# Mixer queries of the second block in reverse order, bias tiles read from one row per head, and masks, constants and first loads placed elsewhere

## The chip, the cores and the metric

The kernel runs on one core of one Trainium2 chip. The metric is the device time of one execution in microseconds, the median of several runs. A core has TensorE (PE, with its weight loads as PEld), VectorE (DVE), ScalarE (ACT), GpSimd (POOL) and SyncE (SP); each runs its own list of instructions in order. DMAs are issued here by SP (weights and some inputs), POOL (small tables, masks, bias tiles) and ACT (one vector table).

## The reference

The input x has 256 rows of 1024 columns. Two blocks follow each other, and each has two layers.

```python
def reference(x, ...):
    x = first_block(x, positions, ...)      # per layer: dilated + stick-breaking attention, gates, conv FFN (2816)
    return second_block(x, mem_2, ...)      # per layer: mixer, cross attention to 256 memory rows, squared-relu MLP (4096)
...
bias = table[t5_bucket(key_pos - query_pos)]            # 28 columns: 8 + 4 + 16 heads
adm  = chunk_id(spos)[None, :] <= chunk_id(tpos)[:, None]
score = einsum('bqhs,bqh->bqs', relu(q_idx . k_idx), w_idx)   # even mixer: picks 64 keys for each query
s = q . k * scale + bias                                 # then masked, softmax, times values
```

The mixer of the second block's layer 0 ("even") has four pairs of heads with a selection of keys (dsa) and two pairs of difference heads (diff); that of layer 1 ("odd") has eight pairs with a band mask and sinks. Every mixer head adds a bias that depends on key position minus query position alone.

## The kernel before

All activations are kept transposed, as tiles of 128 channels by 256 rows of x, and every weight matrix is cut into blocks of up to 512 KB by `plan()`, in the order of their use. `prep` (L188 to L207) loads a block on SP's queue into one of three `raw` buffers, and ACT (L201) and DVE (L202) split it into a high and a low half in fp32r (`w`, eight buffers). A projection is then three matmuls per 128x128 piece (`mm3`: high by high, low by high, high by low). `take` prepares up to `LEAD` blocks ahead of the one in use. The order on each engine is set by a list scheduler at build time (`schedule_with_timeline_sim`); `no_sync(later, earlier)` only forces an order on one engine.

The places that the change touches:

- **Start** (L371 to L404): SP loads x in four tiles, weight block 0 between them, then blocks 1 and 2, the identity `ident`, the masks `m_dil`, `m_sb`, `m_tri`; POOL loads positions, `invf`, `m_chunk`, `m_band`, `table`, `sink`, `lamv`. `Split.chunk` (L267 to L274) scales x by the norm's gain and splits it, ACT the high half and DVE the low. DVE also makes the rope tables from the positions (L616 to L634).
- **The bias table** (`relative_bias`, L639 to L656), called at step j = 1 of the up projection of the first block's layer 0 (L872): one matmul turns the 32x28 table and a one-hot tensor into `brel`, one row of 384 floats per head, which goes to DRAM (`brel_d`). Seven copies of four heads each (L654, paced by a POOL copy at L888 in steps j = 2 to 8) then write every row 128 times with a pitch of 385 into `skew_d`. A bias tile (L486) is a read of `skew_d` with pitch 384, so that partition p sees the row from offset 127 - p on.
- **Bias tiles** (`bias_tile`, L489): DVE adds the mask `m_chunk` (diff heads) or `m_band` (odd heads) to the tile (L494). Tag "bias" has three buffers, of which `m_sb` holds one until the first block's layer 1 has used it.
- **Queries**: `scaled` (L1018) takes a projection out of PSUM with one DVE multiply. Query positions 0 to 127 and 128 to 255 are handled as two tiles (`TILE`). `split_half` (L497) takes an attention result out of PSUM, ACT the high half (L498) and DVE the low (L499).
- **Selection** (`index_scores` L1073, `choose` L1101): weights `wi` (L1063), scores summed in `work` (L1081), then eight rounds of MAX8 and MATCH_REPLACE8 on DVE; `dsa_pair` adds the result to the bias (L1161).
- **Constants of the second block**: the lambda sums (L942) and four copies of the sinks (L953).

Of the kernel before, what the change touches and what calls it, by code (L numbers as in the profile page):

```python
# [19 lines left out]
P = 128  # L20
# [110 lines left out]
def net(ctx, tc, A, out):  # L131
# [116 lines left out]
    class Split:  # L248
# [19 lines left out]
        def chunk(self, k, src, gain, eng=None):  # L268

            if k % 2 == 0:  # L270
                self.new()
            t = self(k)
            act.activation(t[:, 0], src, AF.Copy, scale=gain)
            (eng or dve).scalar_tensor_tensor(t[:, 1], src, gain, f(t[:, 0]), op0=OP.mult, op1=OP.subtract)  # L274
# [122 lines left out]
    ident = const("ident", [P, P])  # L397
# [4 lines left out]
    m_sb = sb("bias", "m_sb")  # L402
    nc.sync.dma_start(m_sb, A["m_sb"])
    m_tri = const("m_tri", [P, 2, P])  # L404
# [190 lines left out]
    for c in range(8):  # L595
        h.chunk(c, x[c // 2][:, c % 2], vcol(V_MIX + c))
# [9 lines left out]
    m_chunk = const("m_chunk", [P, T], nc.gpsimd)  # L606
    m_band = const("m_band", [P, T], nc.gpsimd)
# [3 lines left out]
    lamv = cp.tile([P, 4, 64], F32, name="lamv")  # L611
    nc.gpsimd.dma_start(lamv, A["lambda"].partition_broadcast(P))
# [3 lines left out]
    dve.tensor_copy(posf, pos)  # L616
# [22 lines left out]
    def relative_bias():  # L639
        onehot = sb("p", "onehot", (512,))  # L640
        nc.gpsimd.dma_start(onehot[0:32], A["onehot"])
        ps = bank("ms", "brel", (512,), part=28)
        pe.matmul(ps, table, onehot[0:32], start=True, stop=True)
        brel = sb("p", "brel_s", (512,))
        dve.tensor_copy(brel[0:28], ps)
        bdram = dp.tile([28, 384], F32, name="brel_d")
        nc.gpsimd.dma_start(bdram, brel[0:28, 0:384])

        skew = dp.tile([28, P * 385], F32, name="skew_d")
        def copy(h0, n=4):  # L650
            src = bass.AP(tensor=bdram.tensor, offset=bdram.offset + h0 * 384, ap=[[384, n], [0, P], [1, 384]])
            dst = bass.AP(tensor=skew.tensor, offset=skew.offset + h0 * P * 385,
                          ap=[[P * 385, n], [385, P], [1, 384]])
            return nc.gpsimd.dma_start(dst, src).ins  # L654

        return skew, copy  # L656

    for l in range(DEPTH):
# [38 lines left out]
        if l == 0:  # L697
            nrm = first_sums()
        rc = nrm.cols(0)
# [140 lines left out]
        def residual(w, y, k, gains):  # L840
# [5 lines left out]
            def on_part(c, a, b):  # L846
# [3 lines left out]
                dve.tensor_tensor(t, x[c // 2][:, c % 2], a, op=OP.add)  # L850
# [16 lines left out]
        for j in range(11):  # L867
# [4 lines left out]
            if j == 1 and l == 0:  # L872
                skew, copy = relative_bias()
# [67 lines left out]
    for j in range(2):  # L941
        dve.tensor_tensor_reduce(lprod, lamv[:, 2 * j], lamv[:, 2 * j + 1], 1.0, 0.0, op0=OP.mult, op1=OP.add,  # L942
                                 accum_out=lsum[:, j:j + 1])
# [7 lines left out]
    for m in range(2):  # L951
        for i in range(2):
            dve.tensor_copy(sink4[:, :, 2 * m + i], sink[:, 8 * m:8 * m + 8])  # L953
# [68 lines left out]

    def even(h, nrm):
# [5 lines left out]
        qb, kb = [scaled(o0, r8, "qb")], [scaled(o1, rr, "kb")]  # L1029
# [25 lines left out]
        def index_queries(c):  # L1055
            qi.append(scaled(proj_t("ev_in", c, h), rr, "qi"))
# [7 lines left out]

        def diff_operands(c):
            qb.append(scaled(proj_t("ev_in", c, h), r8, "qb"))
            kb.append(scaled(proj_t("ev_in", c + 256, h), rr, "kb"))

        def dsa_operands(c):
            qa.append(scaled(proj_t("ev_in", c, h), r8, "qa"))  # L1070
# [39 lines left out]
        def diff_pair(hp):  # L1110
# [39 lines left out]
            split_half(on, o_all.pairs[hp][:, :, 0], o_all.pairs[hp][:, :, 1])  # L1150

        def dsa_pair(hp):
# [10 lines left out]
            for n, c in enumerate(COLS):  # L1163
# [9 lines left out]
            split_half(o, t[:, 0], t[:, 1])  # L1173

        pipeline([diff_pair(0), index_keys, "step", lambda: index_queries(776), "step", lambda: index_queries(1032),
                  lambda: diff_values(0), "step", lambda: diff_values(1), "step",
# [7 lines left out]
    def odd(h, nrm):  # L1184
# [5 lines left out]
        qs = [scaled(o1, r8, "qo")]  # L1190
# [7 lines left out]
        def more(j):  # L1198
            qs.append(scaled(proj_t("od_in", 256 * j, h), r8, "qo"))
# [7 lines left out]
        def pair(ch):  # L1207
# [20 lines left out]
            split_half(o, t[:, 0], t[:, 1])  # L1228
# [228 lines left out]
def shape_constants():  # L1457
# [15 lines left out]
    C["m_tri"] = np.stack([np.where(j >= i, -8.0, 0.0), np.full((P, P), -8.0)], axis=1).astype(f4)  # L1473
    C["m_chunk"] = np.where(s // 64 <= t // 64, 0.0, NEG).astype(f4)
# [25 lines left out]
```

## Time and profile before

| | |
|---|---|
| median of 3 runs | 1460.91 us (1459.95 to 1466.13) |
| profiled execution, its own time | 1462.57 us |
| its span | 1460.5 us, so 2.07 us lie outside it |
| PE busy | 1404.1 us, 96% of the span |
| DVE busy | 1015.4 us, 70% |
| ACT busy | 886.0 us, 61% |
| POOL busy | 34.2 us, 2% |
| granted clock of TensorE, mean | 0.988 |
| bytes moved by DMA | 241.62 MB, mean 165 GB/s |

The kernel's work is a row of stages. The first block's layer 0 runs from 0 to some 397 us, its layer 1 to some 767 us with the same program but for loads and set-up, and the two layers of the second block fill the rest. The engines' busy shares are means over all stages; waits are read stage by stage.

### The profile page before, as it was taken

The page shows a single profiled execution, that of the slowest core. Times are in us where ns is not written, and L with a number is a line of the kernel's source. Part 1 is how long each engine was busy: PE and PEld are TensorE (multiplying, and loading weights), DVE is VectorE, ACT ScalarE, POOL GpSimd, SP SyncE. Part 2 cuts the span into 40 slices and gives each one's busy share as a digit, 9 for nine tenths or more (in the row PEclk, how much of TensorE's full clock was granted, in tenths as well). Part 3 has the DMA queues.
Part 4 walks back from the last instruction along what each step waited for, and adds up shares of the span by engine and source line. Part 5 has one row for each costly group of instructions (what it writes and reads, how often), then busy time and mean ns, then how long its engine had stood idle before and what let it go on. Part 6 is the DMA issues. An engine that isn't in the chain of part 4 may idle for free.

```text
span 1460.5 us, 26250 instructions
## 1 busy us (share of the span) xinstructions
PE 1404.1 (96%) x9948; PEld 1274.4 (87%) x9948; DVE 1015.4 (70%) x2135; ACT 886.0 (61%) x1744; POOL 34.2 (2%) x63
## 2 busy tenths in 40 slices
PE   8999999799999999999999998899999999899997
PEld 6789999798888899999999987699989978699986
DVE  6555887567665659888867795687656876677554
ACT  7556665455565566666756656576656676576553
POOL 1000000100000000000000010000000010000000
PEclk9999999899999999999999999999999999999998
DMA  8533666576654345565665554156566534266662
GB/s 263 166 116 106 186 187 213 175 227 198 199 173 147 102 151 178 186 187 186 207 196 160 156 158 132 61 157 186 182 183 185 167 102 131 62 199 188 188 188 87
DMA packets 74447, 241.62 MB, mean 165 GB/s; under 512 B 11663, under 2 KB 16159, under 8 KB 74321
## 3 DMA queue, kind: packets, MB, share of 16 engines
q1 hardware_dynamic: 67568, 230.03, 50.8%
q0 software_dynamic: 6608, 9.74, 2.2%
q8 instruction: 78, 1.28, 0.4%
q14 instruction: 49, 0.39, 0.1%
q10 hardware_dynamic: 144, 0.19, 0.0%
HBM read 238.79 MB, written 6.60 MB: 168 GB/s over the span
## 4 chain that ended last, share of the span: by engine, by line
PE 85%; DMA 6%; DVE 4%; ACT 4%; issue 1%; SPq 0%; POOL 0%; DVEq 0%; ACTq 0%; POOLq 0%
PE mm L231 52%; PE mw L231 21%; DMA raw<-in_wt_dram 4%; PE ssum L427 2%; PE mo L231 1%; DVE w L202 1%; PE sd L734 1%; DMA skew_d<-brel_d 1%; ACT w L201 1%; PE pT L483 1%; PE pv L524 1%; PE sc L586 1%; PE sc L585 1%; PE pv L525 1%; PE pTd L483 1%
## 5 line engine op out<-in xcount | busy, mean ns | idle before, releaser
L202 DVE TENSOR_TENSOR w<-raw,w 128x512 fp32r<-128x512 f32 (+2 forms) x866 | 585.2, 685 | 336.2 <-ACT w L201 327.2
L201 ACT ACTIVATE w<-raw 128x512 fp32r<-128x512 f32 (+2 forms) x866 | 532.2, 625 | 424.4 <-PE mm L231 218.1
L231 PE MATMUL mm<-xh,w 128*128 128x256 f32 x5892 | 723.6, 283 | 20.5 <-DVE fa L885 13.4
L231 PEld LDWEIGHTS mm<-xh,w 128*128 128x128 f32 x5892 | 704.2, 189 | 37.4 <-issue 20.1
L231 PE MATMUL mw<-xh,w 128*128 128x512 f32 (+1 forms) x1832 | 329.3, 340 | 4.6 <-DVE mx L1164 2.5
L231 PEld LDWEIGHTS mw<-xh,w 128*128 128x128 f32 x1832 | 282.1, 189 | 47.7 <-DVE mx L1164 2.9
L231 PE MATMUL mm<-w,xh 128*128 128x512 f32 (+2 forms) x672 | 147.1, 372 | 7.2 <-ACT w L201 7.1
L231 PEld LDWEIGHTS mm<-w,xh 128*128 128x128 f32 x672 | 114.0, 191 | 30.7 <-ACT w L201 8.1
L978 ACT ACTIVATE xh<-x,vec 128x256 fp32r<-128x256 f32 x48 | 22.6, 501 | 11.5 <-DVE x L1333 11.0
L487 POOL DMA_DIRECT2D bias<-skew_d x28 | 15.1, 543 | 611.7 <-DVE nm L535 275.0
L880 ACT ACTIVATE ftt<-fa,vec 128x256 f32<-128x256 f32 x44 | 24.1, 595 | 8.1 <-DVE fa L875 6.9
L231 PE MATMUL mo<-xh,w 128*128 128x256 f32 x192 | 28.0, 288 | 0.5 <-ACT xh L498 0.5
L231 PEld LDWEIGHTS mo<-xh,w 128*128 128x128 f32 x192 | 24.4, 189 | 3.8 <-issue 1.2
L981 DVE SCALAR_TENSOR_TENSOR xh<-x,vec,xh 128x256 fp32r<-128x256 f32 x48 | 22.0, 480 | 1.1 <-ACT xh L978 1.1
L431 ACT ACTIVATE sq<-x 128x512 f32<-128x512 f32 x33 | 20.4, 618 | 2.4 <-DMA x<-in_xT_dram 2.1
L881 DVE SCALAR_TENSOR_TENSOR ftt<-fa,vec,ftt 128x255 f32<-128x255 f32 x44 | 20.9, 483 | 0.7
L882 DVE SCALAR_TENSOR_TENSOR ftt<-fa,vec,ftt 128x254 f32<-128x254 f32 x44 | 21.0, 477 | 0.0
L178 ACT ACTIVATE ftt<-ftt 128x512 f32<-128x512 f32 x22 | 13.9, 631 | 9.9 <-DVE ftt L882 9.9
L265 ACT ACTIVATE xh<-fa 128x512 fp32r<-128x512 f32 x22 | 13.7, 625 | 9.9 <-DVE fa L886 9.8
L734 PE MATMUL sd<-qTs 64*128 64x128 f32 (+1 forms) x96 | 18.8, 350 | 0.0
L438 DVE TENSOR_TENSOR sq<-sq 128x512 f32<-128x512 f32 x26 | 17.8, 686 | 0.0
L1332 DVE TENSOR_TENSOR y<-y,rstd 128x512 f32<-128x512 f32 (+1 forms) x25 | 14.5, 581 | 4.5 <-ACT rstd L178 4.4
(406 smaller groups left out, 1162.6 us busy)
## 6 DMA issues: line engine op xcount, KB each, us to landing
raw<-in_wt_dram SPq DMA_DIRECT2D x411, 512.0 KB, 3.6
raw<-in_wt_dram SPq DMA_DIRECT2D x16, 384.0 KB, 3.5
skew_d<-brel_d POOLq DMA_DIRECT2D x7, 768.0 KB, 16.2
bias<-skew_d POOLq DMA_DIRECT2D x28, 128.0 KB, 3.1
raw<-in_wt_dram SPq DMA_DIRECT2D x4, 520.0 KB, 3.5
mem<-in_memT_dram SPq DMA_DIRECT2D x8, 256.0 KB, 3.7
x<-in_xT_dram SPq DMA_DIRECT2D x4, 256.0 KB, 5.9
raw<-in_wt_dram SPq DMA_DIRECT2D x4, 256.0 KB, 3.4
```

What stands on the lines that cost most here:

```text
L201: act.activation(w[:, 0], raw[:, a:b], AF.Copy)
L202: dve.tensor_tensor(w[:, 1], raw[:, a:b], f(w[:, 0]), op=OP.subtract)
L231: i = pe.matmul(o, a, b, start=start, stop=stop, skip_group_check=True).ins
L427: state["sum"] = pe.matmul(self.ps, ones, s, start=first, stop=last).ins
L431: act.activation(sq, src, AF.Square)
L483: pe.transpose(o, i, ident)
L734: pe.matmul(s[m][:, g - gs[0]], half(qT[g], hp, m)[:, col(i)], half(kT[g], hp, m)[:, :n], start=(g == gs[0]), stop=True, skip_group_check= ...
L880: act.activation(t[:, c], a[:, c], AF.Identity, bias=vcol(vb + V_CB + ch), scale=w[2])
L881: dve.scalar_tensor_tensor(t[:, c, 1:], a[:, c, :T - 1], w[1], t[:, c, 1:], op0=OP.mult, op1=OP.add)
L882: dve.scalar_tensor_tensor(t[:, c, 2:], a[:, c, :T - 2], w[0], t[:, c, 2:], op0=OP.mult, op1=OP.add)
L978: act.activation(hi, t, AF.Copy, scale=g)
L981: return dve.scalar_tensor_tensor(lo, t, g, f(hi), op0=OP.mult, op1=OP.subtract)
```

## The change

- Queries of the mixers are written in reverse order within each tile of 128 (`flip`, a view with a step of -1), in `queries`, which takes the place of `scaled` for `qb`, `qi`, `qa`, `qo`: 10 DVE multiplies. Fourteen pairs of output splits read their source through the same view (`split_flipped`), so the order is natural again after the attention. `m_chunk` and `m_band` are reversed on the host.
- With reversed queries, partition p needs the bias row from offset p on, which is a read of `brel_d` with pitch 1. `skew_d`, its seven copies and the POOL copies that pace them are gone.
- The weights `wi` of the selection have queries on the partitions; a matmul with a new constant `exchange` and a DVE copy reverse them (`flip_index_weights`).
- The mask adds of `bias_tile`, the lambda sums and the sink copies are ordered behind the last residual add of the first block on DVE.
- `m_dil`, `m_sb`, `m_tri`, `m_chunk`, `m_band`, `lamv` are loaded by POOL behind a POOL copy that waits for the last low half of x; weight block 2 goes ahead of `ident`. The first rope instruction is ordered behind the last low half of x on DVE.

```diff
-    m_dil = sb("p", "m_dil", (3, T))
-    nc.sync.dma_start(m_dil, A["m_dil"])
...
+    def flip(t):
+        return bass.AP(tensor=t.tensor, offset=t.offset + P - 1,
+                       ap=[list(d) for d in t.ap[:-1]] + [[P, 2], [-1, P]])
+    def tiles(t):
+        return t.rearrange("p (i t) -> p i t" if len(t.shape) == 2 else "p c (i t) -> p c i t", i=2)
     def bias_load(o, h):
-        src = bass.AP(tensor=skew.tensor, offset=skew.offset + h * P * 385 + 127, ap=[[384, P], [1, T]])
+        src = bass.AP(tensor=brel.tensor, offset=brel.offset + h * 384, ap=[[1, P], [1, T]])
         nc.gpsimd.dma_start(o, src)
...
-            dve.tensor_tensor(t, t, mask[:, None, :].to_broadcast([P, len(heads), T]), op=OP.add)
+            no_sync(dve.tensor_tensor(t, t, mask[:, None, :].to_broadcast([P, len(heads), T]), op=OP.add).ins,
+                    state["block1"])
...
+    def split_flipped(ps, hi, lo):
+        act.activation(tiles(hi), flip(ps), AF.Copy)
+        dve.tensor_tensor(tiles(lo), flip(ps), tiles(f(hi)), op=OP.subtract)
...
-    dve.tensor_copy(posf, pos)
+    no_sync(dve.tensor_copy(posf, pos).ins, split_last)
...
-        skew = dp.tile([28, P * 385], F32, name="skew_d")
-        def copy(h0, n=4):
...
+            held = [pool.tensor_copy(sb("sm", "held", (1,)), f(h(7)[:, 1, 0:1])).ins]
+            def late(t, src):
+                held.append(nc.gpsimd.dma_start(t, src).ins)
+                no_sync(held[-1], held[-2])
+                return t
...
-            if l == 0 and 2 <= j < 9:
-                pace = pool.tensor_copy(sb("sm", "pace", (1,)), a[:, 0, 0:1]).ins
-                no_sync(copy(4 * (j - 2)), pace)
...
+    def queries(o, r, nm):
+        s = single(nm if nm[1] != "b" else "qkb", nm)
+        dve.tensor_tensor(flip(s), tiles(o), tiles(over(r)), op=OP.mult)
...
+        def flip_index_weights():
+            ps = bank("ms", "wf", (16,))
+            pe.matmul(ps, exchange, wi.rearrange("p i h -> p (i h)"), start=True, stop=True)
+            dve.tensor_copy(wi.rearrange("p i h -> p (i h)"), ps)
```

POOL's list around the first block's up projection, before (`pace` is the pacing copy, `fa` a tile of the up projection):

```order
L641 DMA onehot<-in_onehot_dram 32x512
L647 DMA brel_d<-brel_s 28x384
L888 COPY pace<-fa 128x1
L654 DMA skew_d<-brel_d 512x1x384
...
L487 DMA bias<-skew_d 128x256 x2
...
L487 DMA bias<-skew_d 128x256 x16
```

and now, from the start of the program on:

```order
L697 COPY held<-xh 128x1
L702 DMA m_dil<-in_m_dil_dram 128x768
L702 DMA m_sb<-in_m_sb_dram 128x512
L702 DMA m_tri<-in_m_tri_dram 128x256
L702 DMA m_chunk<-in_m_chunk_dram 128x256
L702 DMA m_band<-in_m_band_dram 128x256
L702 DMA lamv<-in_lambda_dram 128x256
L648 DMA onehot<-in_onehot_dram 32x512
L654 DMA brel_d<-brel_s 28x384
L492 DMA bias<-brel_d 128x256 x18
```

The seven skew copies are gone (the first two bias loads stood behind the third of them), and six mask loads have come in ahead.

DVE's list in that up projection before (`fa`, `ftt` and `xh` belong to the projection, `w` to weight blocks):

```order
L494 TENSOR_TENSOR bias<-bias,m_chunk 128x256
L885 TENSOR_TENSOR fa<-mm,rstd 128x512
L202 TENSOR_TENSOR w_2982<-raw_2977,w_2982 128x512
L886 TENSOR_TENSOR fa<-fa,ftt 128x512
L202 TENSOR_TENSOR w_3011<-raw_3009,w_3011 128x512
```

and now at the end of the first block, behind its last residual add (`x` by `rstd` is the norm between the blocks):

```order
L963 COPY sink_8622<-sink 128x8 x4
L499 TENSOR_TENSOR bias<-bias,m_chunk 128x256 x3
L202 TENSOR_TENSOR w_8560<-raw_8555,w_8560 128x512
L952 ISA lp,ls<-lamv 128x64
L952 ISA ls 128x1
L1020 SCALAR_TENSOR_TENSOR x_8662<-x_8032,vec,rstd 128x256
```

Three mask adds, four sink copies and the lambda sums have moved from between the projections to this place.

DVE's list at the selection's start before:

```order
L1063 TENSOR_SCALAR wi<-mm,rcol 128x4
L1081 SCALAR_TENSOR_TENSOR work_8878<-relu,wi,m_chunk 128x128
L1081 SCALAR_TENSOR_TENSOR work_8879<-relu,wi,m_chunk 128x256
L1081 SCALAR_TENSOR_TENSOR work_8878<-relu,wi,work_8878 128x128
L1081 SCALAR_TENSOR_TENSOR work_8879<-relu,wi,work_8879 128x256
```

and now (`wf` is the reversed copy of `wi` in PSUM):

```order
L1078 TENSOR_SCALAR wi<-mm,rcol 128x4
L202 TENSOR_TENSOR w_9263<-raw_9261,w_9263 128x512
L202 TENSOR_TENSOR w_9337<-raw_9335,w_9337 128x512
L1083 COPY wi<-wf 128x16
L202 TENSOR_TENSOR w_9366<-raw_9364,w_9366 128x512
L202 TENSOR_TENSOR w_9369<-raw_9364,w_9369 128x512
L1101 SCALAR_TENSOR_TENSOR work_8860<-relu,wi,m_chunk 128x128
```

The first score sum stands behind the copy out of `wf` and four weight splits.

## Rows read from the trace of the kernel before

**Rows 1.** The page, part 1: busy time, share of the span and instructions.

```profile
PE 1404.1 (96%) x9948; PEld 1274.4 (87%) x9948; DVE 1015.4 (70%) x2135; ACT 886.0 (61%) x1744; POOL 34.2 (2%) x63
```

**Rows 2.** Stretches: length, PE, PEld, DVE, ACT, POOL busy, PE clock, DMA share, GB/s.

```profile
202.00:342.66 140.66, 127.09 (x1024) 124.04 (x1022) 100.36 (x176) 76.96 (x134) 11.41 (x17) 0.96 0.64 197
...
588.00:705.00 117.00, 116.89 (x987) 116.61 (x986) 98.09 (x167) 76.46 (x128) 0.00 (x0) 1.00 0.59 185
```

**Rows 3.** Timeline of PE, layer 0's up projection: start, us, instruction [idle before].

```profile
201.22 0.59 PE L427 MATMUL ssum<-fold,ones 128*128 128x256 f32 x2
...
204.19 1.04 PE L643 MATMUL brel<-onehot,table 32*28 32x512 f32 x2
...
278.25 36.15 PE L231 MATMUL mm<-xh,w 128*128 128x256 f32 x288 [10.42 <-DVE fa L885]
...
334.64 7.84 PE L231 MATMUL mw<-xh,w 128*128 128x512 f32 x43
```

**Rows 4.** Timeline of PE, the same stage of layer 1.

```profile
588.37 0.59 PE L427 MATMUL ssum<-fold,ones 128*128 128x256 f32 x2
...
704.88 5.33 PE L231 MATMUL mw<-xh,w 128*128 128x512 f32 x29
```

**Rows 5.** Waits from 200 to 345 us: total us, times, longest.

```profile
ACT w L201 <- DMA raw<-in_wt_dram: 29.0, 21, 2.7
...
PE mm L231 <- DVE fa L885: 13.4, 3, 10.4
DVE bias L494 <- DMA bias<-skew_d: 12.1, 1, 12.1
```

**Rows 6.** Timeline from 250 to 300 us, POOL and DVE.

```profile
256.41 1.08 POOL L654 DMA_DIRECT2D skew_d<-brel_d  x1
...
273.60 1.14 POOL L487 DMA_DIRECT2D bias<-skew_d  x2 [16.10 <-DMA skew_d<-brel_d]
276.14 0.42 DVE L494 TENSOR_TENSOR bias<-bias,m_chunk 128x256 f32<-128x256 f32 x1 [12.11 <-DMA bias<-skew_d]
```

**Rows 7.** A stretch of the stall, columns as in rows 2.

```profile
272.00:276.00 4.00, 0.00 (x0) 0.00 (x0) 0.00 (x0) 0.00 (x0) 1.14 (x2) 0.50 0.24 70
```

**Rows 8.** DMA issues from 200 to 345 us: KB each, median us to landing.

```profile
skew_d<-brel_d POOLq DMA_DIRECT2D x7, 768.0 KB, 16.2
```

**Rows 9.** Timeline of PE at the start of the program.

```profile
6.12 5.57 PE L231 MATMUL mm<-w,xh 128*128 128x512 f32 x12 [6.12 <-ACT w L201]
12.64 5.37 PE L231 MATMUL mm<-w,xh 128*128 128x512 f32 x22 [0.95 <-ACT w L201]
```

**Rows 10.** Timeline of PE, the first unit of layer 1.

```profile
397.04 11.30 PE L231 MATMUL mm<-w,xh 128*128 128x512 f32 x48
```

**Rows 11.** Timeline of ACT at the start of the program.

```profile
10.64 0.91 ACT L273 ACTIVATE xh<-x,vec 128x256 fp32r<-128x256 f32 x2 [0.39 <-DMA x<-in_xT_dram]
```

**Rows 12.** A stretch at the start, columns as in rows 2.

```profile
12.64:20.00 7.36, 7.36 (x36) 6.18 (x37) 5.33 (x19) 5.91 (x14) 0.00 (x0) 1.00 0.92 311
```

**Rows 13.** Timeline of DVE: sink copies, and the norm between the blocks.

```profile
16.03 0.39 DVE L953 COPY sink<-sink 128x8 f32<-128x8 f32 x4
...
769.96 0.49 DVE L1010 SCALAR_TENSOR_TENSOR x<-x,vec,rstd 128x256 f32<-128x256 f32 x1 [1.50 <-ACT rstd L178]
```

**Rows 14.** Timeline of PE at the end of the selection.

```profile
867.82 0.48 PE L585 MATMUL sc<-ka,qa 64*128 64x128 f32 x2 [1.04 <-DVE mx L1164]
```

**Rows 15.** Instructions of single lines: duration in ns, least, median, most.

```profile
L1081 DVE SCALAR_TENSOR_TENSOR work<-relu,wi,work x14: 343/414/481, 823.9 to 839.0; 128x128 f32<-128x128 f32 x7, 128x256 f32<-128x256 f32 x7
...
L1020 DVE TENSOR_TENSOR qo<-mm,r x4: 681/682/691, 1158.5 to 1174.5; 128x512 f32<-128x512 f32 x4
...
L499 DVE TENSOR_TENSOR xh<-pv,xh x12: 411/418/426, 885.3 to 1212.1; 128x256 fp32r<-128x256 f32 x12
...
L667 DVE TENSOR_TENSOR ra<-nat,trig x24: 215/222/228, 24.9 to 435.8; 128x64 f32<-128x64 f32 x24
```

**Rows 16.** The tile bias: us from issue to landing of its 28 loads.

```profile
DMA to landing us min/median/max: 2.3/3.1/3.9
```

More of the change, by code (lines that the diff above doesn't have):

```diff
@@ L604, in first_sums @@
         return ns
-    m_chunk = const("m_chunk", [P, T], nc.gpsimd)
-    m_band = const("m_band", [P, T], nc.gpsimd)
+    exchange = const("exchange", [P, P], nc.gpsimd)
     table = const("table", [32, 28], nc.gpsimd)
@@ L637, in net, with relative_biases @@
     brel_state = {}
-    def relative_bias():
+    def relative_biases():
         onehot = sb("p", "onehot", (512,))
@@ L647, in relative_bias @@
         nc.gpsimd.dma_start(bdram, brel[0:28, 0:384])
-        skew = dp.tile([28, P * 385], F32, name="skew_d")
-        def copy(h0, n=4):
[L651 to L656, printed above, removed]
+        return bdram
     for l in range(DEPTH):
@@ L697, in net @@
         if l == 0:
+            held = [pool.tensor_copy(sb("sm", "held", (1,)), f(h(7)[:, 1, 0:1])).ins]
+            ident = const("ident", [P, P])
             nrm = first_sums()
+            def late(t, src):
+                held.append(nc.gpsimd.dma_start(t, src).ins)
+                no_sync(held[-1], held[-2])
+                return t
+            m_dil = late(sb("p", "m_dil", (3, T)), A["m_dil"])
+            m_sb = late(sb("bias", "m_sb"), A["m_sb"])
+            m_tri = late(cp.tile([P, 2, P], F32, name="m_tri"), A["m_tri"])
+            m_chunk = late(cp.tile([P, T], F32, name="m_chunk"), A["m_chunk"])
+            m_band = late(cp.tile([P, T], F32, name="m_band"), A["m_band"])
+            lamv = late(cp.tile([P, 4, 64], F32, name="lamv"), A["lambda"].partition_broadcast(P))
         rc = nrm.cols(0)
@@ L872, in net @@
             if j == 1 and l == 0:
-                skew, copy = relative_bias()
+                brel = relative_biases()
             a = sb("ft", "fa")
@@ L941, in net @@
     for j in range(2):
-        dve.tensor_tensor_reduce(lprod, lamv[:, 2 * j], lamv[:, 2 * j + 1], 1.0, 0.0, op0=OP.mult, op1=OP.add,
-                                 accum_out=lsum[:, j:j + 1])
+        no_sync(dve.tensor_tensor_reduce(lprod, lamv[:, 2 * j], lamv[:, 2 * j + 1], 1.0, 0.0, op0=OP.mult,
+                                         op1=OP.add, accum_out=lsum[:, j:j + 1]).ins, state["block1"])
     actf(lsum, lsum, AF.Exp)
@@ L952, in net @@
         for i in range(2):
-            dve.tensor_copy(sink4[:, :, 2 * m + i], sink[:, 8 * m:8 * m + 8])
+            no_sync(dve.tensor_copy(sink4[:, :, 2 * m + i], sink[:, 8 * m:8 * m + 8]).ins, state["block1"])
     def in_order(made):
@@ L1172, in dsa_pair @@
             t = o_all.pairs[2 + hp // 2][:, hp % 2]
-            split_half(o, t[:, 0], t[:, 1])
+            split_flipped(o, t[:, 0], t[:, 1])
         pipeline([diff_pair(0), index_keys, "step", lambda: index_queries(776), "step", lambda: index_queries(1032),
-                  lambda: diff_values(0), "step", lambda: diff_values(1), "step",
+                  lambda: diff_values(0), "step", lambda: diff_values(1), flip_index_weights, "step",
                   lambda: index_scores(0), lambda: index_scores(1), lambda: diff_operands(2312),
@@ L1473, in shape_constants @@
     C["m_tri"] = np.stack([np.where(j >= i, -8.0, 0.0), np.full((P, P), -8.0)], axis=1).astype(f4)
+    C["exchange"] = np.ascontiguousarray(np.eye(P, dtype=f4)[::-1])
+    t = t[::-1]
     C["m_chunk"] = np.where(s // 64 <= t // 64, 0.0, NEG).astype(f4)
```

30 lines of the change are left out of this document (13 added, 17 removed).

## The prediction

> **What bounds the kernel now.** I read the page's busy times first [rows 1]. PE is busy for 1404.1 of 1460.5 us, so the reader is to see that time can only come from the 56 us in which PE stands, from matmuls that run slowly, or from matmuls that go away; the change removes no matmul and adds one. Next I looked for a stage that has a twin. The first block runs the same program in both layers, and the stretches of the two up projections differ [rows 2]: in layer 1 PE is busy for all but 0.1 us at a granted clock of 1.00, in layer 0 it lacks 13.6 us, at 0.96. The two timelines of PE give the size. Both stages begin with the same row sum and then do 977 projection matmuls; layer 0 needs 334.64 - 201.22 = 133.42 us for this [rows 3], layer 1 704.88 - 588.37 = 116.51 [rows 4]. Layer 0 thus loses 16.91 us, of which 1.04, taken as 1.0, is the bias table's own matmul, which stays.
>
> The waits say where the rest is from [rows 5]: PE waits 13.4 us for `fa` of DVE, three times, 10.4 of it at once. DVE itself waits 12.1 us at L494, the mask add of a bias tile, and ACT waits 29.0 us for weight blocks. One chain explains the largest wait [rows 6]: the fourth skew copy is issued at 256.4, POOL's next instruction, a bias load, has to wait 16.1 us for it, lands some 2.5 us later, and the mask add that the scheduler had put into DVE's list between the up projection's instructions starts at 276.1 only. Behind it on DVE stand `fa` and the weight splits, and PE restarts at 278.25. In this stall the granted clock falls to 0.50, the 1.2 GHz level [rows 7], and the first matmuls behind it run at it. The skew copies take 16.2 us each, seven times [rows 8], while ACT waits for weights.
>
> **The change, part by part.**
>
> *Skew copies and mask adds (the main term).* The seven copies go, and the list of POOL shows bias loads right behind the write of `brel_d`, 18 in a row. The mask adds stand behind the first block. So both causes of the chain are gone at once, and layer 0 should run like its twin: 116.5 + 1.0 = 117.5 in place of 133.4, a gain of **15.9 us**. The twin also loads four memory tiles of 256 KB, so nothing in it is lighter on DMA. What is late next in this stage is what is late in the twin: nothing that stops PE for more than 0.1 us. Removing the seven pacing copies from POOL is worth nothing in itself, since nothing but the copies waits for them. Bounds: 12.1 us if only the DVE wait goes, 16.9 if the table's matmul hides as well.
>
> *Start.* The first 12 matmuls take 6.12 to 12.64 [rows 9], 6.52 us, where the twin does 48 in 11.30 [rows 10], so 12 in 2.83. The loss is 3.7 us and the most that can be gained. The 13th matmul waits for ACT's split of weight block 1, ACT does the last two chunks of x just before, and these wait for their DMA until 10.64 [rows 11]. Ahead of or beside x the change takes out `m_chunk`, `m_band` and `lamv`, 128 KB each, and puts in `exchange`, 64 KB: 0.33 MB less, 1.05 us at the 311 GB/s of the next stretch [rows 12]. I take a gain of **0.9 us**, since the chain behind x (two activations and a square) stays. The larger masks stood on SP behind block 2 and held back block 3; they now go onto POOL's queue after the last low half of x, some 11 us in, and are needed only in the attention after five units of projection. The stretch from 12.64 to 20 moves 311 GB/s with the engines 92% busy [rows 12], so the 1.18 MB that come in there are not free: they take 3.8 us of DMA time from weight blocks 3 to 6, which before was taken ahead of block 3. I put the balance at nothing, with ends of -2.8 us (the whole 3.7 is won) and +2.9 (3.8 us of starving less the 0.9).
>
> The Trainium skill speaks against a gain from the other queue: DMA: Bandwidth & Descriptors, section "Issuing engines are not separate DMA queues", says that DMAs of all issuers run on the same 16 engines and interleave. By it the masks get their share at once instead of waiting behind blocks, so the start would win nothing and the sum would be 14.8 in place of 15.7. What the row shows is a DMA share of 0.92, which is compatible with both.
>
> *DVE at the end of the first block.* Three mask adds of 0.42 [rows 6], four sink copies that take 0.39 together [rows 13], and two lambda sums (over 64 columns, taken at 0.3 each, the 0.22 of a 64-element multiply [rows 15] and a read) are 2.25 us; between the last residual add and the norm DVE stands idle for 1.50 us, waiting for ACT's `rstd` [rows 13]. So some 0.7 us come onto the chain to the next operand; PE has a projection of the memory keys in hand then. I take **+0.3**, between 0 and 0.8. These instructions took the same time earlier, in stages where DVE was not the limit, so nothing is credited there.
>
> *Reversing `wi`.* One matmul of 16 columns beside the 1.04 us of one of 512 [rows 3]: **+0.2** (0 to 1.0). The copy out of PSUM delays the first score sum: the list shows four weight splits and the copy ahead of it now. Behind it on DVE is the whole selection, and PE waits for the first dsa scores to be consumed at its end, 1.04 us already [rows 14], so what the selection loses is paid in full. By my count of the list, two more of the 16 score sums (0.41 each [rows 15]) stand behind the last operand of the second diff pair, less some idle time that they fill: **+0.6**, between 0 and +4 (the whole delay of the first sum, four splits and a copy, unabsorbed).
>
> *Reversed views.* 10 multiplies of 0.68 us and 14 pairs of splits, 12 of 128x256 (0.42 on DVE [rows 15]) and two of twice that. No row has a step of -1. The nearest is the rope's multiply, which walks short runs inside 64-column heads: 0.222 us for 64 elements, against 0.418 for 256 contiguous ones [rows 15], or 1.02 ns for an element, with no more fixed time than 0.16. Broken runs thus cost nothing, and I take **0**. A gain is excluded, as no element falls away. The upper end is half rate: 0.26 us for each 256 elements on DVE and as much on ACT, over 16 such units (12 + 2 x 2), 8.4 us if all lies on the path.
>
> *Bias loads.* Same bytes, same count; they land in 2.3 to 3.9 us [rows 16]. New is that the 128 rows of a tile overlap in 1.5 KB of DRAM. The skew copies read 6 KB over and over and moved 768 KB in 16.2 us [rows 8], 2.7 for 128 KB. I take 0 change, between -1 (all at 2.3 on some path) and +2.7 each for about three loads that DVE waits for, +8.
>
> Sum: -15.9 - 0.9 + 0.3 + 0.2 + 0.6 = **-15.7 us**. Against the profiled execution that is 1462.57 - 15.7 = 1446.9. That execution lies 1.66 above the median, so the forecast of the median is 1460.91 - 15.7 = **1445.2 us**.
>
> **The rivals.**
> - *The new waits eat part of it.* The start starves (+2.9 for -0.9) or the selection pays 4 us: 1449 to 1452. For it speaks that DVE works with hardly a gap through the selection; against it that the scheduler has filled the new gap with splits.
> - *Slow overlapping reads or reversed reads at half rate*: +8 or +8.4, 1453 to 1454, which is about the bound of no change. For it only that no row shows these; against it the rope's rows.
> - *Slower than before: the reversed reads of PSUM run at a quarter of the rate.* Each 256 elements then cost 0.78 us more on each of ACT and DVE, 25 us over the 16 units, at the ends of both mixers where PE waits for each split: 1470. It decides from 15.7 / 16 = 0.98 us a unit on, some 2.9 times the streaming time. Against it stands the slope above. The Trainium skill, Advanced Engine Details and Errata, section "Memory Cachelines", says that PSUM lines hold two fp32 values and that non-contiguous patterns slow matmuls; a reversed run still uses both values of a line, so by its letter this rival needs more than the rule, and no row here shows a case.
> - *The change doesn't do what it says*: the 13.4 us of PE's waits come from something else in layer 0, and only the start changes: 1460. The chain in rows 6 and the list of DVE, where the mask adds have left the up projection, speak against it.
>
> **How the numbers follow.** My forecast, within 4 us either way, 0.72; the eaten gain 0.11; slow reads, half on either side of the bound, 0.08; no effect 0.05; slower 0.04. About 0.5% (7.3 us, so below 1453.6) is what a measurement of this kernel tells from no change. Faster: 0.72 + 0.11 + 0.04 = 0.87; same: 0.04 + 0.05 = 0.09; slower: 0.04. The range goes from 1439, where the start wins all of its 3.7 (2.8 more), the table's matmul hides (1.0), the three small costs vanish (1.1) and loads land early (1), to 1451.5, most of the first rival.
>
> **What would show it.** In the profile after, PE's stretch from the row sum to the down projection takes some 117.5 us, no wait at the mask add is over 1 us, ACT's waits for weights there fall from 29 to almost nothing, and the clock stays at 1.00. The 13th matmul starts near 11.7. The selection ends within 1 us of its old distance from the last `wi`. Reversed multiplies stay at 0.68 and splits at 0.42. It would be wrong if layer 0 stayed above 125, if splits took over 0.7, or if PE gained a wait of over 3 us in the even mixer.

## The result, and the profile after

The changed kernel takes 1446.01 us (median of 4 runs, 1445.13 to 1446.97) against 1460.87 us beside it: a ratio of 0.9893, 95% interval 0.9875 to 0.9911, so 13 to 18 us less. The forecast was 1445.2, its range 1439.0 to 1451.5. The profiled execution has a span of 1444.2 us and takes 1446.04 in all.

Part 1 of the page of the changed kernel, as [rows 1]:

```profile
PE 1400.5 (97%) x9950; PEld 1271.1 (88%) x9950; DVE 1017.2 (70%) x2136; ACT 889.0 (62%) x1744; POOL 26.7 (2%) x54
```

PE is busy for 3.6 us less with two more records of matmuls. Most of this lies in the two up projections of the first block: in layer 0's PE is busy for 116.63 us in place of 120.03, partly because no matmul runs at the lower clock behind a stall any more, as the prediction has it; in layer 1's it is busy for 114.84 in place of 116.40, which no term of the prediction foresaw. The stage of the main term, and its twin in layer 1, as stretches (length, PE, PEld, DVE, ACT, POOL busy, PE clock, DMA share, GB/s), as [rows 2]:

```profile
202.09:318.72 116.63, 116.63 (x986) 115.55 (x984) 98.22 (x167) 76.32 (x128) 1.64 (x3) 1.00 0.60 187
571.58:686.55 114.97, 114.84 (x983) 114.56 (x982) 97.20 (x166) 76.06 (x128) 0.00 (x0) 1.00 0.60 188
```

PE's timeline at the two ends of the first, as [rows 3]:

```profile
202.09 0.59 PE L422 MATMUL ssum<-fold,ones 128*128 128x256 f32 x2
...
205.05 1.04 PE L650 MATMUL brel<-onehot,table 32*28 32x512 f32 x2
...
318.72 6.49 PE L231 MATMUL mw<-xh,w 128*128 128x512 f32 x36
```

And the longest waits from 200 to 330 us, as [rows 5] (total, times, longest):

```profile
POOL brel_d L654 <- DVE brel_s L652: 90.2, 1, 90.2
ACT w L201 <- PE mm L231: 38.1, 61, 1.2
DVE w L202 <- ACT w L201: 15.8, 22, 1.2
```

The stage fell from 133.42 to 116.63 us, PE has no gap in it, and the clock stays at 1.00. ACT no longer waits for DMA (29.0 us before); it waits for PE to give back the weight buffers, so PE is now the bound. POOL's 90 us are idle time of an engine with nothing to do.

Cut at PE's own marks, the two profiled spans compare like this (us; a stage lasts until the next mark). A row sum is the matmul `ssum` of a norm; layer 1's first one comes inside its first projections, so these stand with layer 0's down projection:

| stage | before | after | difference |
|---|---|---|---|
| to the first dilated score | 63.04 | 64.26 | +1.22 |
| layer 0, to the up projection's row sum | 138.18 | 137.83 | -0.35 |
| layer 0's up projection | 133.42 | 116.63 | -16.79 |
| layer 0's down projection, to layer 1's first row sum | 79.06 | 78.52 | -0.54 |
| layer 1, to the up projection's row sum | 174.67 | 174.34 | -0.33 |
| layer 1's up projection | 116.51 | 114.97 | -1.54 |
| layer 1's down projection, to the boundary's row sum | 61.96 | 61.92 | -0.04 |
| boundary, to the first mixer's row sum | 21.99 | 22.14 | +0.15 |
| first mixer, to the cross scores | 135.19 | 136.13 | +0.94 |
| from there to the end of the span | 536.48 | 537.46 | +0.98 |
| sum | 1460.5 | 1444.2 | -16.3 |

So one stage explains the size. Four questions stay open: how much of its gain comes from the copies and how much from the wait; why layer 1's up projection, the same list of instructions, lost 1.54 us; whether the start really lost 1.2; and what slows the mixer.

### The profile page after: what moved, and what is told of

Read it like the earlier page. It is cut to its first block, busy times and chain, and to the rows that moved or that the text cites. A ratio compares the mean times of both kernels' runs of the same rounds, so it can differ in the third digit from the quotient of the medians.

```text
span 1444.2 us, 26236 instructions
## 1 busy us (share of the span) xinstructions
PE 1400.5 (97%) x9950; PEld 1271.1 (88%) x9950; DVE 1017.2 (70%) x2136; ACT 889.0 (62%) x1744; POOL 26.7 (2%) x54
## 4 chain that ended last, share of the span: by engine, by line
issue 53%; PE 38%; DVE 3%; ACT 3%; DMA 1%; POOL 0%; SPq 0%; DVEq 0%; POOLq 0%; ACTq 0%
PE mm L231 20%; PE mw L231 12%; PE ssum L422 1%; PE mo L231 1%; PE pT L478 1%; ACT w L201 1%; PE pv L534 1%; PE sc L595 1%; PE sc L596 1%; DVE w L202 1%; PE pv L535 1%; DMA bias<-brel_d 1%; ACT sq L426 0%; DMA x<-in_xT_dram 0%; ACT px L178 0%
## 5 line engine op out<-in xcount | busy, mean ns | idle before, releaser
L492 POOL DMA_DIRECT2D bias<-brel_d x28 | 15.0, 539 | 689.9 <-DVE sbb L809 297.6
L898 DVE TENSOR_TENSOR fa<-mm,rstd 128x512 f32<-128x512 f32 x22 | 15.1, 687 | 3.1 <-PE mm L231 3.1
```

The lines of the kernel that those rows point to most:

```text
L898: dve.tensor_tensor(a, o, over(rr), op=OP.mult)
```

## The experiments

Each ratio below is to the kernel before as measured beside that run (1460.87 to 1463.47 us), so ratios compare across runs better than times do.

**How well do stages repeat?** The changed kernel again, without an edit.

> The changed kernel once more, as it is, to learn how far its stages repeat from one profiled execution to the next. Theory (stage times repeat, so that 1 us is a real difference): time 1446.0 within 0.9, row sum of layer 0's up projection at 202.1 within 0.3, that stage 116.6 within 0.3, the even mixer from its first projection to the cross attention 150.4 within 0.3. Rival (stages scatter by a microsecond of themselves): these move by 1 us or more, and the 1.54 us by which layer 1's up projection was shorter than before (114.97 for 116.51, the same program) comes back.

Measured: 1447.44 us (1444.72 to 1448.92), ratio 0.9892 (0.9875 to 0.9910). Its two up projections:

```profile
203.29:319.92 116.63, 116.63 (x985) 115.55 (x984) 98.25 (x167) 76.33 (x128) 1.63 (x3) 1.00 0.60 187
572.80:687.76 114.96, 114.84 (x983) 114.56 (x982) 97.20 (x166) 76.05 (x128) 0.00 (x0) 1.00 0.60 187
```

These stages repeat within 0.01 us, so the 1.54 us of layer 1 are real. Other stages don't repeat, and the expectations of the time and of the row sum (203.29 in place of 202.1) missed: the first dilated score came 1.2 us later (65.47 for 64.26), and the first cross attention took 43.41 for 41.56. Its stretch in the first profile, then in the repetition:

```profile
906.74:948.30 41.56, 34.15 (x228) 28.15 (x229) 27.27 (x63) 21.73 (x54) 0.00 (x0) 0.92 0.21 65
```

```profile
907.65:951.06 43.41, 36.02 (x229) 30.21 (x230) 27.36 (x63) 21.92 (x54) 0.00 (x0) 0.88 0.24 66
```

The granted clock differs, 0.92 and 0.88, where PE stands idle for 7 us. Nothing under 2 to 3 us should be read from one profile of the start or of a stage in which PE waits and the clock moves.

**The wait or the copies?** Two kernels take the main term apart, both from the kernel before. The first moves the mask adds alone:

```diff
-            dve.tensor_tensor(t, t, mask[:, None, :].to_broadcast([P, len(heads), T]), op=OP.add)
+            no_sync(dve.tensor_tensor(t, t, mask[:, None, :].to_broadcast([P, len(heads), T]), op=OP.add).ins,
+                    state["block1"])
```

> The kernel before with one edit: the mask adds of the bias tiles are ordered behind the first block's last residual add; the seven skew copies stay. Theory (the copies cost mostly through the mask add that waits on DVE, 12.1 of the 16.9 us, and the rest through weight blocks that come late): layer 0's up projection takes 121.3 us (133.4 - 12.1), the time falls by some 12 to 1449. Rival (the copies take the DMA engines from the weights, and the wait at the add only hid that): ACT's waits for weight blocks stay at some 29 us and the stage stays above 128, the time above 1455. Other rival (the add was all of it): the stage takes 117.5.

The second takes out the copies and leaves the adds early:

```diff
-        src = bass.AP(tensor=skew.tensor, offset=skew.offset + h * P * 385 + 127, ap=[[384, P], [1, T]])
+        src = bass.AP(tensor=brel.tensor, offset=brel.offset + h * 384, ap=[[1, P], [1, T]])
...
-            if l == 0 and 2 <= j < 9:
-                pace = pool.tensor_copy(sb("sm", "pace", (1,)), a[:, 0, 0:1]).ins
-                no_sync(copy(4 * (j - 2)), pace)
```

> The kernel before without the seven skew copies and the POOL copies that pace them, and with bias tiles read straight from the row; queries are not reversed, so the bias of the second block's first mixer and of its second is put on the wrong queries: the reversal is left out. The mask adds stay early. Theory (the copies and the wait behind them are the whole of the main term): layer 0's up projection takes 117.5 us in place of 133.4 and the time falls by 16 us below the kernel before, to some 1445; the reversed views cost nothing. Rival (the early adds still wait for their loads on DVE): the stage takes 119 or more. Rival (reversed views do cost): this kernel is faster than the changed one by 2 us or more beyond what the start and the reversal of the weights (together some 1 to 2 us) give.

Measured: adds late 1453.17 us, ratio 0.9942 (0.9922 to 0.9962); no copies 1449.68 us, ratio 0.9909 (0.9888 to 0.9930). The stage with the adds late, as a stretch:

```profile
203.32:327.10 123.78, 118.48 (x985) 116.39 (x984) 92.88 (x161) 70.42 (x123) 11.00 (x17) 1.00 0.69 216
```

its waits from 202 to 330 us:

```profile
ACT w L201 <- DMA raw<-in_wt_dram: 27.5, 18, 2.7
POOL bias L487 <- DMA skew_d<-brel_d: 15.2, 1, 15.2
```

and what became of PE's long stall, on PE's timeline:

```profile
288.31 5.84 PE L231 MATMUL mm<-xh,w 128*128 128x256 f32 x48 [0.70 <-DVE fa L876]
294.92 11.50 PE L231 MATMUL mm<-xh,w 128*128 128x256 f32 x96 [0.78 <-DVE fa L886]
307.95 11.61 PE L231 MATMUL mm<-xh,w 128*128 128x256 f32 x96 [1.53 <-DVE fa L886]
321.35 5.92 PE L231 MATMUL mm<-xh,w 128*128 128x256 f32 x48 [1.79 <-DVE fa L886]
```

Both stages of the kernel without copies:

```profile
204.05:321.61 117.56, 117.56 (x985) 116.48 (x984) 98.92 (x169) 76.40 (x128) 1.63 (x3) 1.00 0.59 186
574.85:691.29 116.44, 116.33 (x983) 116.05 (x982) 97.98 (x166) 76.32 (x128) 0.00 (x0) 1.00 0.59 185
```

and the wait of its early mask adds, from 203 to 322 us:

```profile
DVE bias L494 <- DMA bias<-brel_d: 0.2, 1, 0.2
```

With the adds late the 10.4 us stall is gone, POOL still waits 15 us for the copies but nobody waits for POOL, and the stage takes 133.42 - 123.78 = 9.64 us less. ACT still waits 27.5 us for weights, and that now reaches PE as a row of stalls of 0.5 to 1.8 us behind `fa`. Without copies the stage takes 117.56: these waits go too, another 6.22 us, and the early adds wait for no more than 0.2 us. So copies are the cause of both shares, 9.6 through the add on DVE and 6.2 through late weights, and moving the adds is worth nothing once they are gone. The expectations of 121.3 and of above 128 both missed: some of the weights' lateness had hidden under the stall. Both times lie above those expected, by 4 us (1449) and by 5 (1445). In the profile without copies the start is 2.84 us longer than in the profile before, and the mixer and what follows 1.8 longer, in stages that scatter by as much. The kernel without copies reverses nothing, and its ratio of 0.9909 is no better than the 0.9906 of the changed kernel with `xh` at its old place (below), so reversed views cost no time that shows.

**The start.** Two kernels: the changed one with the start of before, and the changed one with the six mask loads held until the first unit's projection is out of PSUM (`L697` waits for `nats[1]` in place of `h(7)`).

```diff
-            held = [pool.tensor_copy(sb("sm", "held", (1,)), f(h(7)[:, 1, 0:1])).ins]
-            ident = const("ident", [P, P])
...
+    m_dil = sb("p", "m_dil", (3, T))
+    nc.sync.dma_start(m_dil, A["m_dil"])
+    m_sb = sb("bias", "m_sb")
+    nc.sync.dma_start(m_sb, A["m_sb"])
```

> The changed kernel with the start of the kernel before: masks and constants where they were on the two queues, identity ahead of weight block 2, the rope's first instruction not held. Theory (the moved masks take DMA time from weight blocks at 13 to 20 us and cost the start some 0.9 us): the row sum of layer 0's up projection comes at 201.2 in place of 202.1, its stage stays at 116.6, the time is 1445.1. Rival (what the start lost comes from something else, such as the first bias loads or the list of the attention): the row sum stays at 202.1 and the time at 1446.0. If the new start is a gain after all, the row sum comes later than 202.1.

> The changed kernel with the six mask loads held back further: behind the evacuation of the first unit's projection in place of the last low half of x. Theory (they collide with weight blocks 3 to 6 at 13 to 20 us): ACT's wait for a weight block of 6.4 us at 22.5 shrinks, the row sum of layer 0's up projection comes at 201 or earlier, since the part of the new start that helps (smaller loads ahead of x) is kept; time 1444.5 to 1445.2. Rival (the bytes cost the same wherever they fall while weights stream): the row sum stays at 202.1 within 0.3, time 1446.0.

Measured: start of before 1449.95 us, ratio 0.9915 (0.9899 to 0.9930); masks later 1446.42 us, ratio 0.9891 (0.9874 to 0.9909). The old start did not bring the time down. It went up, because both up projections went back to 117.56 and 116.44. Holding the masks longer did nothing that can be told; the row sum comes at 202.73, not at 201, and the wait of 6.4 us that it was to shrink had been 2.5 in the repetition of the changed kernel already.

With all runs of this study the start can be averaged. The first dilated score, in five profiles with the old start (before, and the runs with adds late, without copies, with the old start, and with the old start and `xh` low): 63.04, 65.14, 65.88, 63.90, 65.60, mean 64.7. In eight with the new one: 64.26, 65.47, 65.68, 63.47, 64.29, 65.06, 65.56, 64.07, mean 64.7. My theory of a lost microsecond, formed on one profile of each, falls: the start is worth nothing that shows above its scatter of 2 to 3 us.

**Why the up projections got faster.** In the run with the old start they are slow, in all with the new start fast, and the list of PE in layer 1's stage is the same. What differs is an address. Pools give space to tags in the order of their first use, and the old start allocates `m_dil` and `m_sb` ahead of the tiles `xh` of x, the new one behind. So, by the addresses in the built programs, `xh` begins at byte 83072 of a partition in place of 107328 (107840 with the constant `exchange`). One kernel puts `xh` back up in the changed kernel, one puts it down under the old start; no load moves in either.

```diff
     prep(2)
     state["next"] = 3
+    m_dil = sb("p", "m_dil", (3, T))
+    m_sb = sb("bias", "m_sb")
...
-            m_dil = late(sb("p", "m_dil", (3, T)), A["m_dil"])
+            m_dil = late(m_dil, A["m_dil"])
```

> The changed kernel with one edit that moves no load: the tiles of two masks are allocated where the kernel before allocated them, so the tiles xh of x in the first block lie 24.8 KB higher in each partition, as they did before. Theory (where xh lies sets the pace of the up projection's matmuls: 114.97 us in layer 1 with xh low, 116.5 with xh high, in all profiles so far): layer 1's up projection goes back to 116.5, layer 0's from 116.6 to 117.6, the time rises by some 2.5 to 1449. Rival (the pace comes from something else in the new start, such as which buffers the weights use): both stages stay at 115.0 and 116.6 and the time at 1446.5.

> The changed kernel with the start of the kernel before (as in the run with that start), but with the tiles xh allocated ahead of the two masks, so that they lie low as in the changed kernel; all loads keep their order. Theory (the old start is worth some 1.2 us and xh's place some 2.5, one against the other in the run with the old start): layer 0's row sum comes at 201 to 202, the up projections take 116.6 and 115.0, the time is some 1.2 below the changed kernel, 1444.8 to 1445.5. Rival (the old start is worth nothing): the time is that of the changed kernel, 1446 to 1447.5.

Measured: `xh` high 1448.79 us, ratio 0.9906 (0.9889 to 0.9922); old start with `xh` low 1446.77 us, ratio 0.9894 (0.9876 to 0.9913). Both stages with `xh` high:

```profile
201.67:319.24 117.57, 117.57 (x985) 116.49 (x984) 98.58 (x167) 76.50 (x128) 1.63 (x3) 1.00 0.60 186
572.47:688.97 116.50, 116.38 (x983) 116.10 (x982) 98.04 (x166) 76.31 (x128) 0.00 (x0) 1.00 0.60 185
```

and with the old start and `xh` low:

```profile
203.31:319.94 116.63, 116.63 (x986) 115.55 (x984) 98.25 (x167) 76.35 (x128) 1.63 (x3) 1.00 0.60 187
572.79:687.79 115.00, 114.89 (x983) 114.61 (x982) 97.24 (x166) 76.12 (x128) 0.00 (x0) 1.00 0.60 187
```

The place alone switches the pace. In the run with the old start and `xh` low only `xh` goes back down: the other tiles that the early masks push up (squares, row sums, small vectors) stay up, and the stage is fast all the same. The place also accounts for the two stages ahead of the up projections: 138.2 and 174.7 us in every profile with `xh` high, 137.7 to 137.8 and 174.3 low. Together that is some 0.35 + 0.93 + 0.33 + 1.5 = 3.1 us of the gain. The second run also shows no gain of the old start alone: its ratio is all but that of the changed kernel (0.9893), and nothing is to be seen of the expected 1.2 us, though the interval is wider than that.

Two more kernels set `xh` between, by allocating one of the two tiles early:

> The changed kernel with only one mask's tile allocated early, so that the tiles xh lie 6 KB higher (from byte 89216 of a partition, not 83072). Theory (where xh lies sets the pace, 115.0 us for layer 1's up projection from 83072 and 116.5 from 107840): the stage takes 115.0 or 116.5 here, or a value between if it grows with the distance (then 115.4). Rival (it hangs on the order in which tiles are allocated, not on the place): 115.0 or 116.5 here and in the next run alike, with no relation to the distance.

> The changed kernel with only the other mask's tile allocated early, so that the tiles xh lie 18 KB higher (from byte 101696). Theory (the pace grows with the distance): layer 1's up projection takes 116.1 us. Rival (a step at some address): 115.0 or 116.5, which says on which side of this address the step lies.

One run each, of 1447.38 and 1454.57 us; the second is also longer in the start, in the mixer and behind it, so only the stage is read here. Layer 1's up projection from byte 89216, then from byte 101696:

```profile
572.36:687.37 115.01, 114.88 (x983) 114.60 (x982) 97.22 (x166) 76.05 (x128) 0.00 (x0) 1.00 0.60 187
```

```profile
574.56:691.05 116.49, 116.38 (x983) 116.10 (x982) 98.03 (x166) 76.30 (x128) 0.00 (x0) 1.00 0.60 185
```

It is a step, not a slope: two places are fast, two are slow, nothing lies between. What the matmul meets at the slow places isn't shown; no run here separates the candidates.

**The mixer.** Three kernels from the changed one: without the reversal of the weights, with that reversal in two halves, and with bias rows that don't overlap in DRAM.

```diff
-                  lambda: diff_values(0), "step", lambda: diff_values(1), flip_index_weights, "step",
+                  lambda: diff_values(0), "step", lambda: diff_values(1), "step",
```

> The changed kernel without the matmul and the copy that reverse the selection's weights; the reversal of these weights is left out. Theory (the reversal delays the selection: the first score sum stood 7.8 us later in the mixer than before, the last 2.2 and the selection's end 2.0): the selection's end moves back to some 93.1 us behind the mixer's first projection (before 93.1, after 95.1), the mixer takes 149.3 in place of 150.4, the time falls by 1 to 1445.0. Rival (the mixer lost its 1.1 us through bias loads that land later or through the clock): the selection's end may move, but the mixer stays at 150.4 and the time at 1446.0.

```diff
-            pe.matmul(ps, exchange, wi.rearrange("p i h -> p (i h)"), start=True, stop=True)
+            pe.matmul(ps, exchange, wi[:, :, hs], start=True, stop=True)
```

> The changed kernel with the reversal of the selection's weights done in two halves, the first behind the first projection of values, so that the first score sums don't wait for the second. Theory (the single reversal costs the selection 0.4 us): the first score sum stands 34.5 to 35.5 us behind the mixer's row sum in place of 42.0, the selection ends at 65.5 in place of 65.9, the time is 0.4 below the changed kernel, 1445.6 to 1447. Rival (the score sums then fill DVE where weight splits stood, and the end doesn't move): the selection ends at 65.9.

```diff
-        src = bass.AP(tensor=brel.tensor, offset=brel.offset + h * 384, ap=[[1, P], [1, T]])
+        src = bass.AP(tensor=wt.tensor, offset=wt.offset + h * P * 384 + 127, ap=[[384, P], [1, T]])
```

> The changed kernel with the rows of a bias tile read from 128 separate places (pitch 384 floats) of an array in DRAM that holds weights, in place of 128 overlapping places of one row; the bias itself is left out by this, and the loads no longer wait for the write of the row. Theory (overlapping reads land later and hold up DVE at the mixer's start, 3.5 us in place of 2.4): landings go back from 3.1/3.5/5.1 us (least, median, most) to 2.3/3.1/3.9, the wait at the mask add to 2.4, the selection ends 64.9 us after the mixer's row sum in place of 65.9 (64.5 before, and 0.4 for the reversal of the weights), time 1 us below the changed kernel. Rival (the later landing has to do with where the load stands in the queue or what else moves then): landings and the wait stay within 0.2, the selection ends at 65.9.

Measured: without the reversal 1447.46 us, ratio 0.9895 (0.9879 to 0.9910); in halves 1447.92 us, ratio 0.9901 (0.9886 to 0.9916); rows apart 1444.16 us, ratio 0.9878 (0.9861 to 0.9894). (The selection's end of 65.9 in the last two expectations is the first score of a dsa pair, 14 us ahead of the end that PE waits for; the table has both.) From the mixer's row sum, in us:

| | first score sum | first dsa score | selection's end | cross scores |
|---|---|---|---|---|
| before | 34.37 | 64.54 | 78.99 | 135.19 |
| no copies, nothing reversed | 35.47 | 65.65 | 80.09 | 135.88 |
| changed, weights not reversed | 35.20 | 65.46 | 79.95 | 135.63 |
| changed | 41.99 | 65.92 | 80.86 | 136.13 |
| changed, in halves | 35.37 | 66.05 | 80.54 | 138.73 |
| changed, rows apart | 40.63 | 64.57 | 79.59 | 133.64 |

The selection's end is the wait of [rows 14]. In the changed kernel PE waits half a microsecond longer there:

```profile
851.47 0.92 PE L595 MATMUL sc<-ka,qa 64*128 64x128 f32 x3 [1.58 <-DVE mx L1184]
```

The eight profiles whose mixer is that of the changed kernel have the selection's end at 80.78 to 81.01 and the cross scores at 135.84 to 138.66; the two with the mixer of before have 78.99 and 79.03, and 135.19 and 133.95. So the table's third column can be read to 0.2 us and its last one not. The halves bring the first sum back to 35.4, and the end moves by 0.3 only, so the sums fill time that splits had filled. Of the 1.87 us that the selection ends later, 0.9 is the reversal (80.86 - 79.95) and 1.0 was there without it. That other microsecond is the first load of the mixer, a bias tile that POOL can issue only when a buffer comes free. DVE's timeline before, in the changed kernel, and with rows apart:

```profile
802.92 0.43 DVE L494 TENSOR_TENSOR bias<-bias,m_chunk 128x256 f32<-128x256 f32 x1 [2.44 <-DMA bias<-skew_d]
```

```profile
785.69 0.43 DVE L499 TENSOR_TENSOR bias<-bias,m_chunk 128x256 f32<-128x256 f32 x1 [3.53 <-DMA bias<-brel_d]
```

```profile
784.38 0.43 DVE L500 TENSOR_TENSOR bias<-bias,m_chunk 128x256 f32<-128x256 f32 x1 [2.17 <-DMA bias<-in_wt_dram]
```

The landings of all bias loads (us, least, median, most), changed and then rows apart; before they were as in [rows 16]:

```profile
DMA to landing us min/median/max: 3.1/3.5/5.1
```

```profile
DMA to landing us min/median/max: 2.3/2.9/7.1
```

Rows that overlap in DRAM land later, and on the one load that nothing hides this costs DVE 1.1 us. What in them costs the time (the overlap itself, starts only 4 bytes apart, or one small region) these runs don't separate. (The 7.1 belongs to the early loads, which in that run no longer wait for the row's write.) What the later end of the selection costs in time is not shown: the kernels without the reversal and with it in halves were both expected to be faster and are not, and the stretch from the selection's end to the cross scores cannot be read as finely: it takes 54 to 58 us in these kernels, with the granted clock falling here in one place and there in another (to 0.51 from 851.5 to 855 us in the changed kernel).

## Why the prediction was right

*Main term, -15.9: right, and by the right mechanism.* With `xh` where it was, the stage takes 117.56 us (run without copies), forecast 117.5. The chain in [rows 6] held: the copies held POOL, POOL the bias load, the load DVE, DVE PE. (The copy issued at 256.4, which the prediction calls the fourth, is the third; the two before it were issued at 230.75 and 243.31.) The remaining 0.93 of the 16.79 in the stage is the place of `xh`.

*A term that is missing: -3.1.* I took layer 1's up projection for a fixed measure, [rows 4]. It moved by 1.54 itself. The step that failed is "layer 0 should run like its twin: 116.5 + 1.0": the twin's own 116.5 hung on where `xh` lay. I compared work and loads ("nothing in it is lighter on DMA"), not addresses, and a reordered start moves addresses.

*Start, -0.9: not borne out.* Old and new start are alike within their scatter. The 13th matmul, forecast near 11.7 us, starts at 12.98 and in the repetition at 13.27 (12.64 before). My weighing put 1.05 us of lighter traffic ahead of x and called the masks behind it even. The Trainium skill's rule (DMA: Bandwidth & Descriptors, "Issuing engines are not separate DMA queues") gave no gain, and the runs agree with it in this: 64.7 on average in both.

*Boundary, +0.3: the moved instructions cost nothing.* The adds, sinks and sums stand at the place forecast:

```profile
749.39 0.39 DVE L963 COPY sink<-sink 128x8 f32<-128x8 f32 x4
749.69 1.09 DVE L499 TENSOR_TENSOR bias<-bias,m_chunk 128x256 f32<-128x256 f32 x3
...
751.59 0.48 DVE L1020 SCALAR_TENSOR_TENSOR x<-x,vec,rstd 128x256 f32<-128x256 f32 x1
```

The last row no longer waits for `rstd`, where it waited 1.50 [rows 13]: the moved instructions fill that wait. It starts 3.12 us behind the boundary's row sum, as before, so the step that put 0.7 us onto the chain failed. The +0.15 of the table goes with the place of `xh`: the boundary takes 21.99 us in every profile with `xh` high, in three of them with all these instructions moved, and 22.13 to 22.17 in every one with `xh` low.

*Reversal of the weights, +0.2 and +0.6: 0.9 at the selection's end.* Right in size and place. That it "is paid in full" is not shown: without the reversal the time is 1447.46 us, with it 1447.44 in the runs beside.

*Reversed views, 0: right.* A multiply, which writes its result in reverse, and a split, which reads its source in reverse, take what they took [rows 15]:

```profile
L1035 DVE TENSOR_TENSOR qo<-mm,r x4: 681/683/684, 1141.0 to 1157.3; 128x512 f32<-128x512 f32 x4
...
L509 DVE TENSOR_TENSOR xh<-pv,xh x12: 415/418/426, 866.2 to 1194.4; 128x256 fp32r<-128x256 f32 x12
```

So the slower rival, a quarter of the rate, is out: a split of 256 reversed fp32 values of PSUM takes 0.418 us, as forward.

*Bias loads, 0: undersized, +1.1.* I took no change because the skew copies, which read the same 6 KB over and over, moved 128 KB in 2.7 us [rows 8]; a long copy doesn't tell when a short load lands. The bound held (up to 2.7 for each load that DVE waits for), and of the three such loads that I counted one is exposed.

Added up from what the runs separate: -15.9 (copies) - 3.1 (place) - 0.5 (layer 0's down projection, 79.06 with copies and 78.57 without) + 0.15 (boundary) + 0.9 (reversal of the weights) + 1.1 (bias load; both as at the selection's end) = -17.35, against -16.3 in the two profiled spans and -14.9 between the medians, and inside the 13 to 18 of the interval. The start and the stages after the mixer differ by 2.2 in these two profiles, which is scatter. The sum of -15.7 came out close because the main term was right and, by luck, the misses lay against each other: 3.1 of gain not seen, 0.9 that the start didn't give, 1.1 for the load.

None of the kernels that compute the whole result beats the changed one by more than its interval: masks later 0.9891, old start with `xh` low 0.9894, the changed kernel itself 0.9892 in its second measurement. The run with rows apart has the lowest ratio, 0.9878, but its interval overlaps with that of the changed kernel; that a private copy of the bias rows would save time is not shown beyond the 1.3 us at the selection's end (79.59 for 80.86).

## What to carry to other kernels

Look for a twin of the stage, the same program without the suspected work: it priced the main term to 0.1 us, as long as `xh` lay in the same place. Before a microsecond is read out of one profile, profile the same program twice; here some stages repeat to 0.01 us and others, where PE waits and the clock moves, only to 2 or 3. And when an edit changes the order in which tiles are allocated, a stage that it never touched can change its pace, so compare addresses before looking for a wait.

## What was unexpected in the hardware

- The same matmuls on the same data run 1.3% slower when the tiles that they stream lie at byte 101696 or 107840 of a partition than at 83072 or 89216: 116.5 for 115.0 us over some 980 matmuls, at a granted clock of 1.00, with PE busy throughout. The lists of ACT and DVE hold the same work there. The Trainium skill (SBUF — State Buffer, "SBUF: two separate sides") says that on the engines' side only one port pair, which VectorE shares with GpSimd, can be contended; POOL does nothing in that stretch (0.00 busy), so by that rule nothing there should hold up PE's reads at either place, and here PE is slower at one of them. Why is open.
- A load of 128 KB whose 128 rows of 1 KB overlap within 1.5 KB of DRAM lands in 3.5 us (median of 28); with rows at separate places it takes 2.9 to 3.1.
- Walking runs of 128 fp32 values backwards costs nothing here: reading 256 of them from PSUM takes DVE 0.418 us and ACT 0.384 in the splits, and writing 512 to SBUF takes DVE 0.683 in the multiply, all as forwards.
